# Two-layer hybrid encoder on one core: order of the branch projections, of the recurrence's levels and of the split-precision products

## The chip, the cores and the metric

The kernel runs on one core of a Trainium2 chip. The metric is the device time of one execution in microseconds (us). Engines are named as the profile names them: PE is the matrix engine (PEld its weight loads), DVE the vector engine, ACT the scalar engine, POOL the general-purpose engine, SP the engine that issues the weight transfers.

## The reference

256 tokens of width 1024 pass two layers. Each layer is: a half-step SwiGLU feed-forward (width 2816), a mixer, a second half-step feed-forward, each behind an RMS norm and with a residual add. The mixer, cut to what matters here:

```
z = h @ W_in            # u | q | f | v | out-gate (512 each) | branch gates (2 x 1024)
pool_out = pooling mixer of u        # 4 groups, windows 2, 4, 8, 16
o        = HGRN2 recurrence(q, f, v) # 4 heads, 128x128 state
hgrn_out = rmsnorm(o) * silu(out-gate)
merged = sigmoid(gA) * (pool_out @ w_pool_proj) + sigmoid(gB) * (hgrn_out @ w_hgrn_proj)
x = x + merged @ w_out
```

All of it is float32.

## The kernel before, in words

**Split products.** Every weight chunk (128 partitions x 2048 or 1408 columns of float32) is brought in by one transfer on SP's queue and split in two: ACT rounds it to `hi` (L116), DVE forms the rest `lo` = raw - hi (L117), each in two halves. Activations are split likewise, so that `x[:, 0]` is the rounded part and `x[:, 1]` the rest. A product of one 128x128 block is then two matmuls: `hi` against both parts of x at once (512 columns, L161) and `lo` against the rounded part (256 columns, L162). `mm_wide` issues this pair, so highs and lows alternate. `raw` has four buffers, `hi` and `lo` three each; `weights(key)` readies chunks up to two ahead of the one it returns.

**By tokens.** Value, out-gate, branch gates and the two branch projections are computed with tokens on the partitions (`by_tokens`, L185): for each of four k blocks and each half of the tokens (128), three matmuls of 512 columns (L192 to L194), into two accumulators, one for each half. A chunk is 24 matmuls.

**Stages of a layer.** Feed-forward: 22 gate/up chunks of 16 pairs, each followed by its evacuation into `hidden`, then 8 column blocks `j` of the down projection, 22 pairs each in two weight chunks. Mixer: f, v, q; then twelve steps (L606: two of the pool input u, two of the out-gate, eight of the branch gates), one weight chunk each; then the branch projections pp0, pp1, hp0, hp1 (`pp` for the pool branch, `hp` for the recurrence's, the number is the half of the 1024 columns); then the out-projection `wo`, whose first half takes k blocks 0 to 3 of four column blocks, then k blocks 4 to 7.

**Recurrence.** Eight parts: the first level, levels 2 to 64, and `across`. Each scales queries and keys on DVE (`decayed`, L463, L464), updates two decay tables on POOL (L466, L467), multiplies on PE (L484, L496, L510) into a tile of the two-buffer pool `gr`, and keeps a masked part (DVE L474). The scaled operands `m` have two buffers. Before, two parts stand ahead of each of the first four steps, and `outputs` (the final products L585, L587, norm, gate, and transposes L601 into the split tile `yhl`, for one half of the tokens after the other) ahead of step 5.

**From a branch projection to `wo`.** hp0 and hp1 yield, for each half of the tokens: z = ps * gate (L640), z += mg (L641, mg being the gated pp result, L632), four transposes (L601), a split (ACT L223, DVE L224). hp0 makes k blocks 0 to 3 of `merged`, hp1 k blocks 4 to 7.

**What sets the order.** A planner orders the instructions of each engine when the program is built: by priority, which is program order, among those that it holds ready. `urgent()` puts instructions 300 places ahead. So the order on an engine can depart from the order of the code; it is fixed once the program runs, and each engine then works strictly in it. Weight chunks come in the order of the list `stream` (L77).

Of the kernel before, what the change touches and what calls it, by code (L numbers as in the profile page):

```python
# [62 lines left out]
def _body(ctx, tc, a, out):  # L63
# [14 lines left out]
    for l in range(L):  # L78
        def ffn_chunks(f):
            for m in range(KF):  # L80
                stream.append(((f, l, "gu", m), a["gu"][l * 2 + f, m], CH))
            for j in range(KD):
                for h in range(2):
                    stream.append(((f, l, "dn", j, h), a["dn"][l * 2 + f, j][:, h * HALF:(h + 1) * HALF], HALF))
        ffn_chunks(0)
        for i in (0, 1):
            stream.append((("f", l, i), a["wi"][l, i], CH))
        def token_chunks(name, b):
            for i in (0, 1):
                stream.append(((name, l, i), a["wt"][l, b, i], CH))  # L90
        token_chunks("v", 0)
        for i in (2, 3, 4, 5):
            stream.append((("qu"[(i - 2) // 2], l, i % 2), a["wi"][l, i], CH))
        token_chunks("og", 1)
        for b in range(4):
            token_chunks(f"gate{b}", 2 + b)
        for name in ("pp", "hp"):
            for i in range(2):
                stream.append(((name, l, i), a[name][l, i], CH))
        for i in range(4):  # L100
            stream.append((("wo", l, i), a["wo"][l, i], CH))
        ffn_chunks(1)
# [55 lines left out]
    def mm_wide(ps, w, sl, x, start, stop):  # L158
# [2 lines left out]
        mm(ps, wh[:, sl], x, start=start, stop=False)  # L161
        mm(ps[:, 0], wl[:, sl], x[:, 0], start=False, stop=stop)  # L162

    def pair(w):

        pss = [pmm.tile([P, 2, S], F32, tag="mm", name="ps") for _ in range(2)]
        for k in range(KD):
            for g in range(2):
                c = (k * 2 + g) * P
                mm_wide(pss[g], w, slice(c, c + P), xs(k), k == 0, k == KD - 1)  # L170
        return pss

    def pair_sum(pss):
# [11 lines left out]
    def by_tokens(pss, w, x, ks, nk):  # L185

        wh, wl = w
        for i, k in enumerate(ks):
            sl = slice(i * 512, i * 512 + 512)
            for h in range(2):  # L190
                th = slice(h * P, h * P + P)
                mm(pss[h], x(k)[:, 0, th], wh[:, sl], start=k == 0, stop=False)  # L192
                mm(pss[h], x(k)[:, 0, th], wl[:, sl], start=False, stop=False)  # L193
                mm(pss[h], x(k)[:, 1, th], wh[:, sl], start=False, stop=k == nk - 1)  # L194
# [137 lines left out]
    def ffn(l, f, sq, gain):  # L332
        hs = slots(range(11), F32R)

        def hidden(k):
            return hs[k // 2].rearrange("p (k two) s -> p k two s", two=2)[:, k % 2]

        def gate_up(ms):
            ws = [weights((f, l, "gu", m)) for m in ms]
            pss = [[pmm.tile([P, 2, S], F32, tag="mm", name="ps") for _ in range(2)] for _ in ms]  # L340
            for k in range(0, KD, 2):
                for w, ps in zip(ws, pss):
                    for kk in (k, k + 1):
                        for g in range(2):
                            c = (kk * 2 + g) * P
                            mm_wide(ps[g], w, slice(c, c + P), xs(kk), kk == 0, kk == KD - 1)
            return list(zip(ms, pss))

        def evacuate(m, pss):
            z = pair_sum(pss)  # L350
            tt(out=z, in0=z, in1=bc(rb, 2), op=ALU.mult)  # L351
            s = tmp.tile([P, S], F32, tag="s", name="s")
            gate = nc.scalar.activation(s, z[:, 0], AF.Silu)  # L353
            h = tmp.tile([P, S], F32, tag="h", name="h")
            tt(out=h, in0=s, in1=z[:, 1], op=ALU.mult)  # L355
            split([hidden(m)[:, 0], hidden(m)[:, 1]], h)
            return gate

        n = FIRST if (l, f) == (0, 0) else 1
        groups = [range(n)] + [[m] for m in range(n, KF)]  # L360
        wait = gate_up(groups[0])
        with urgent():
            rc = norm_columns(sq)
        rb = None
        for ms in groups[1:]:
            wait += gate_up(ms)
            if rb is None:
                rb = norm_row(rc)
            for m, ps in wait:
                gate = evacuate(m, ps)  # L370
            wait = []
            if (f, m) == (0, 6):
                poolw = act.tile([P, NH, P], F32, tag="poolw", name="poolw")
                nc.sync.dma_start(out=poolw, in_=a["pw"][:, l])
                hnb = act.tile([P, 512], F32, tag="hnb", name="hnb")
                nc.sync.dma_start(out=hnb, in_=a["hnb"][:, l])
                pw.append((poolw, hnb))
            if (l, f, m) == (0, 0, 6):
                with tc.issue_after(gate.ins):
                    lower_bounds()  # L380
                nc.sync.dma_start(out=tab, in_=a["tab"])
        sq = Squares(gain is None)
        for j in range(KD):
            ps = pmm.tile([P, 2, S], F32, tag="mm", name="ps")
            wide = gain is not None or j < KD - 1
            for h in range(2):
                w = weights((f, l, "dn", j, h))
                for k in range(KF // 2):
                    kk = h * (KF // 2) + k
                    (mm_wide if wide else mm3)(  # L390
                        ps if wide else ps[:, 0], w, slice(k * P, k * P + P), hidden(kk), kk == 0, kk == KF - 1)
            if wide:
                with urgent():
                    nc.vector.scalar_tensor_tensor(  # L394
                        out=xT[:, j], in0=ps[:, 1], scalar=0.5, in1=xT[:, j], op0=ALU.mult, op1=ALU.add)
            residual(j, ps[:, 0], 0.5, gain, sq)
        return sq

    def mixer(l, sq, gain):
# [78 lines left out]

        def first_level():
            decayed(1, None, qx[:, :, P:].rearrange("p e (c n) -> p e c n", n=1))  # L480
            for q in range(NH):
                ps = pgr.tile([P, 2, 192], F32, tag="gr", name="gps")
                for g in range(2):
                    mm(ps[:, g], blocks(kk_)[:, 2 * q + g], qx[:, 2 * q + g], start=g == 0, stop=True,  # L484
                       skip_group_check=True)
                e = slice(2 * q, 2 * q + 2)
                tt(out=at_[:, e], in0=ps[:, :, 0:P], in1=ident.unsqueeze(1).broadcast_to([P, 2, P]), op=ALU.mult)
                keep(e, 1, ps[:, :, P:], P)

        def level(n):  # L490
            m = tmp.tile([P, 2 * NH, P], F32, tag="m", name="m")
            decayed(n, *halves(m, n))
            rows = P - n
            ps = pgr.tile([P, 2 * NH, 64], F32, tag="gr", name="gps")
            for e in range(2 * NH):
                mm(ps[0:rows, e], m[:, e, 0:rows], halves(m, n)[1][:, e], start=e == 0, stop=True,  # L496
                   skip_group_check=True)
            if n < 64:
                keep(slice(0, 2 * NH), n, ps[0:rows], rows)
            else:  # L500
                nc.scalar.copy(out=at_[0:64, :, 64:], in_=ps[0:64])

        def across():
            m = tmp.tile([P, 2 * NH, P], F32, tag="m", name="m")
            ml, mr = m[:, 0:NH], m[:, NH:]
            tt(out=ml, in0=kk_[:, :, 0:P], in1=suf[:, :, 0:P], op=ALU.mult)
            tt(out=mr, in0=queries.rearrange("p (h b) t -> p h b t", b=2)[:, :, 1], in1=pre[:, :, P:], op=ALU.mult)
            ps = pgr.tile([P, NH, P], F32, tag="gr", name="gps")
            for h in range(NH):
                mm(ps[:, h], ml[:, h], mr[:, h], start=h == 0, stop=True, skip_group_check=True)  # L510
            nc.scalar.copy(out=ax, in_=ps)


        up = act.tile([P, NH, PAD + S], F32, tag="up", name="up")
# [92 lines left out]
        steps += [lambda b=b, i=i: gate(b, i) for b in range(4) for i in range(2)]  # L607
        recur = [first_level] + [lambda n=n: level(n) for n in LEVELS[1:]] + [across]
        pools = [lambda g=g: pool_group(g) for g in range(NH)]
        for i, st in enumerate(steps):  # L610
            with urgent():
                for f in recur[2 * i:2 * i + 2]:
                    f()
                if i == 5:
                    outputs()
            st()
            if 3 <= i < 7:
# [9 lines left out]
        for b in range(2):  # L627
# [2 lines left out]
            by_tokens(pss, weights(("pp", l, b)), lambda k: part(phl, k), range(4), 4)  # L630
            for h in range(2):
                tt(out=mg[h][:, cols], in0=pss[h], in1=sg[h][:, cols], op=ALU.mult)  # L632
        for b in range(2):
            cols = slice(512 * b, 512 * b + 512)
            pss = token_tiles()
            by_tokens(pss, weights(("hp", l, b)), lambda k: part(yhl, k), range(4), 4)
            with urgent():
# [96 lines left out]
```

## Time and profile before

| | |
|---|---|
| median of 3 runs | 1105.19 us (1105.16 to 1106.74) |
| the profiled execution | 1106.67 us, its span 1104.9 us |
| PE busy | 1079.8 us (98%) |
| PEld busy | 937.1 us (85%) |
| DVE busy | 812.4 us (74%) |
| ACT busy | 573.3 us (52%) |
| POOL busy | 149.1 us (13%) |
| HBM read | 195.41 MB, 178 GB/s over the span |

A matmul's row lasts longer than its turn, since matmuls are pipelined: the distance from one start to the next is what it costs. "idle before" is the time that an engine sat without work, and the name behind the arrow is what ended it.

### The profile page before, as it was taken

The page shows a single profiled execution, that of the slowest core. Times are in us where ns is not written, and L with a number is a line of the kernel's source. Part 1 is how long each engine was busy: PE and PEld are TensorE (multiplying, and loading weights), DVE is VectorE, ACT ScalarE, POOL GpSimd, SP SyncE. Part 2 cuts the span into 40 slices and gives each one's busy share as a digit, 9 for nine tenths or more (in the row PEclk, how much of TensorE's full clock was granted, in tenths as well). Part 3 has the DMA queues.
Part 4 walks back from the last instruction along what each step waited for, and adds up shares of the span by engine and source line. Part 5 has one row for each costly group of instructions (what it writes and reads, how often), then busy time and mean ns, then how long its engine had stood idle before and what let it go on. Part 6 is the DMA issues. An engine that isn't in the chain of part 4 may idle for free.

```text
span 1104.9 us, 15670 instructions
## 1 busy us (share of the span) xinstructions
PE 1079.8 (98%) x6054; PEld 937.1 (85%) x6054; DVE 812.4 (74%) x1221; ACT 573.3 (52%) x984; POOL 149.1 (13%) x144
## 2 busy tenths in 40 slices
PE   8999999999998999999999999999999899999996
PEld 7888888888887888888888888888888688888885
DVE  8887766788656887776677776768985768777653
ACT  6665544643443665554555554446335446555541
POOL 5000001147200200000100000110751011000010
PEclk9999999999998999999999999999999989999998
DMA  9655466544434565546655544675434435554461
GB/s 339 240 183 179 147 188 229 204 153 163 152 128 149 193 214 189 178 135 187 241 198 184 188 155 132 210 266 191 153 120 163 175 115 197 190 191 154 140 197 38
DMA packets 33050, 197.46 MB, mean 179 GB/s; under 512 B 3792, under 2 KB 3920, under 8 KB 15824
## 3 DMA queue, kind: packets, MB, share of 16 engines
q1 hardware_dynamic: 32400, 195.84, 51.6%
q8 instruction: 47, 0.77, 0.3%
q10 hardware_dynamic: 576, 0.64, 0.2%
q14 instruction: 27, 0.22, 0.1%
HBM read 195.41 MB, written 1.05 MB: 178 GB/s over the span
## 4 chain that ended last, share of the span: by engine, by line
PE 85%; DVE 9%; issue 2%; POOL 1%; DMA 1%; ACT 0%; SPq 0%; POOLq 0%; DVEq 0%; ACTq 0%
PE ps L161 49%; PE ps L162 25%; DVE lo L117 5%; PE ps L192 3%; PE ps L193 3%; PE ps L194 3%; DVE m L464 1%; POOL b L467 1%; DMA xT<-in_x 1%; DMA raw<-in_gu 1%; POOL b L466 1%; DVE z L640 0%; DVE m L463 0%; PE gps L585 0%; PE gps L601 0%
## 5 line engine op out<-in xcount | busy, mean ns | idle before, releaser
L161 PE MATMUL ps<-xs__96,hi 128*128 128x512 f32 x1600 | 559.5, 395 | 3.1 <-DVE xs__96 L230 3.1
L117 DVE TENSOR_TENSOR lo<-raw,hi 128x1024 fp32r<-128x1024 f32 (+3 forms) x412 | 463.1, 1159 | 90.9 <-ACT hi L116 90.0
L116 ACT CAST hi<-raw 128x1024 fp32r<-128x1024 f32 (+3 forms) x412 | 374.2, 956 | 196.9 <-issue 81.1
L162 PE MATMUL ps<-xs__96,lo 128*128 128x256 f32 x1600 | 445.7, 280 | 0.0
L161 PEld LDWEIGHTS ps<-xs__96,hi 128*128 128x128 f32 x1600 | 299.3, 187 | 72.7 <-DVE xs__96 L230 4.3
L162 PEld LDWEIGHTS ps<-xs__96,lo 128*128 128x128 f32 x1600 | 301.6, 189 | 1.5 <-DVE lo L117 0.3
L161 PE MATMUL ps<-b,hi 128*128 128x512 f32 x810 | 287.5, 400 | 8.2 <-DVE b L224 8.2
L162 PE MATMUL ps<-b,lo 128*128 128x256 f32 x810 | 226.7, 281 | 0.0
L161 PEld LDWEIGHTS ps<-b,hi 128*128 128x128 f32 x810 | 153.9, 191 | 44.7 <-DVE b L224 8.6
L178 ACT COPY zl<-ps 128x256 f32<-128x256 f32 x200 | 73.4, 371 | 182.0 <-PE ps L162 181.2
L162 PEld LDWEIGHTS ps<-b,lo 128*128 128x128 f32 x810 | 154.7, 191 | 0.5
L253 POOL TENSOR_TENSOR acc<-acc,sq 128x256 f32<-128x256 f32 x48 | 46.9, 977 | 773.5 <-issue 517.7
L179 DVE TENSOR_TENSOR z<-ps,zl 128x256 f32<-128x256 f32 x200 | 83.0, 421 | 45.6 <-ACT zl L178 44.9
L193 PE MATMUL ps<-lo,xs__96 128*128 128x512 f32 x192 | 76.7, 400 | 0.0
L192 PE MATMUL ps<-hi,xs__96 128*128 128x512 f32 x192 | 75.4, 394 | 0.0
L194 PE MATMUL ps<-hi,xs__96 128*128 128x512 f32 x192 | 75.1, 391 | 0.0
L351 DVE TENSOR_TENSOR z<-z,rb 128x512 f32<-128x512 f32 x88 | 60.2, 686 | 0.6 <-ACT rb L284 0.5
L353 ACT ACTIVATE s<-z 128x256 f32<-128x256 f32 x88 | 36.7, 420 | 21.2 <-DVE z L351 21.1
L394 DVE SCALAR_TENSOR_TENSOR xT<-ps,xT 128x256 f32<-128x256 f32 x31 | 13.1, 424 | 45.5 <-PE ps L162 45.5
L223 ACT CAST b<-h 128x256 fp32r<-128x256 f32 x88 | 36.1, 411 | 13.4 <-DVE h L355 13.4
L192 PEld LDWEIGHTS ps<-hi,xs__96 128*128 128x128 f32 x192 | 36.1, 188 | 7.6
L194 PEld LDWEIGHTS ps<-hi,xs__96 128*128 128x128 f32 x192 | 36.1, 188 | 7.1
(123 smaller groups left out, 735.7 us busy)
## 6 DMA issues: line engine op xcount, KB each, us to landing
raw<-in_gu SPq DMA_DIRECT2D x82, 1024.0 KB, 4.8
raw<-in_dn SPq DMA_DIRECT2D x64, 704.0 KB, 4.1
raw<-in_wt SPq DMA_DIRECT2D x24, 1024.0 KB, 4.8
raw<-in_wi SPq DMA_DIRECT2D x12, 1024.0 KB, 4.8
raw<-in_wo SPq DMA_DIRECT2D x8, 1024.0 KB, 4.9
raw<-in_gu SPq DMA_DIRECT2D x8, 512.0 KB, 5.8
raw<-in_pp SPq DMA_DIRECT2D x4, 1024.0 KB, 4.8
raw<-in_hp SPq DMA_DIRECT2D x4, 1024.0 KB, 4.9
```

Source lines behind the costliest of these rows:

```text
L116: nc.scalar.copy(out=hi[:, sl], in_=raw[:, sl])
L117: tt(out=lo[:, sl], in0=raw[:, sl], in1=hi[:, sl].bitcast(F32), op=ALU.subtract)
L161: mm(ps, wh[:, sl], x, start=start, stop=False)
L162: mm(ps[:, 0], wl[:, sl], x[:, 0], start=False, stop=stop)
L178: nc.scalar.copy(out=zl[:, g], in_=pss[g][:, 1])
L179: tt(out=z[:, g], in0=pss[g][:, 0], in1=zl[:, g], op=ALU.add)
L192: mm(pss[h], x(k)[:, 0, th], wh[:, sl], start=k == 0, stop=False)
L193: mm(pss[h], x(k)[:, 0, th], wl[:, sl], start=False, stop=False)
L194: mm(pss[h], x(k)[:, 1, th], wh[:, sl], start=False, stop=k == nk - 1)
L253: nc.gpsimd.tensor_add(out=self.acc, in0=self.acc, in1=sq)
L351: tt(out=z, in0=z, in1=bc(rb, 2), op=ALU.mult)
L353: gate = nc.scalar.activation(s, z[:, 0], AF.Silu)
```

## The change

Four things are reordered; no product is added or taken away. The branch projections go pp0, hp0, pp1, hp1, in the code and in the order of the weight stream. `by_tokens` runs all k blocks of one half of the tokens, then the other half. `wide_run` issues all high products of a chunk and then all low ones; it is used by `pair` (f, q, u), by the down projection and by the gate/up chunks, but not by the first six chunks of the kernel's first feed-forward, and not by `wo`. In the recurrence each part is cut in a scaling and its products, and the products stand one step after the scaling: one part a step over steps 0 to 8, with `outputs` ahead of step 9.

```diff
-        for name in ("pp", "hp"):
-            for i in range(2):
+        for i in range(2):
+            for name in ("pp", "hp"):
                 stream.append(((name, l, i), a[name][l, i], CH))
...
+    def wide_run(w, tiles):
+
+        wh, wl = w
+        for ps, c, x, start, _ in tiles:
+            mm(ps, wh[:, c:c + P], x, start=start, stop=False)
+        for ps, c, x, _, stop in tiles:
+            mm(ps[:, 0], wl[:, c:c + P], x[:, 0], start=False, stop=stop)
...
-        for k in range(KD):
-            for g in range(2):
-                c = (k * 2 + g) * P
-                mm_wide(pss[g], w, slice(c, c + P), xs(k), k == 0, k == KD - 1)
+        wide_run(w, [(pss[g], (k * 2 + g) * P, xs(k), k == 0, k == KD - 1) for k in range(KD) for g in range(2)])
...
-        for i, k in enumerate(ks):
-            sl = slice(i * 512, i * 512 + 512)
-            for h in range(2):
-                th = slice(h * P, h * P + P)
+        for h in range(2):
+            th = slice(h * P, h * P + P)
+            for i, k in enumerate(ks):
+                sl = slice(i * 512, i * 512 + 512)
                 mm(pss[h], x(k)[:, 0, th], wh[:, sl], start=k == 0, stop=False)
...
+            if len(ms) == 1 and ((l, f) != (0, 0) or ms[0] > 5):
+                order = [(k, g) for k in range(KD) for g in range(2)]
+                wide_run(ws[0], [(pss[0][g], (k * 2 + g) * P, xs(k), k == 0, k == KD - 1) for k, g in order])
+                return list(zip(ms, pss))
...
+                kks = [(k, h * (KF // 2) + k) for k in range(KF // 2)]
+                if wide:
+                    wide_run(w, [(ps, k * P, hidden(kk), kk == 0, kk == KF - 1) for k, kk in kks])
+                    continue
...
+        products = None
         for i, st in enumerate(steps):
             with urgent():
-                for f in recur[2 * i:2 * i + 2]:
-                    f()
-                if i == 5:
+                if products:
+                    products()
+                products = recur[i]() if i < len(recur) else None
+                if i == 9:
                     outputs()
             st()
...
-        for b in range(2):
-            cols = slice(512 * b, 512 * b + 512)
             pss = token_tiles()
             by_tokens(pss, weights(("hp", l, b)), lambda k: part(yhl, k), range(4), 4)
```

## Rows read from the trace of the kernel before

**Rows 1.** The page: busy us, share of the span and instructions of each engine.

```profile
PE 1079.8 (98%) x6054; PEld 937.1 (85%) x6054; DVE 812.4 (74%) x1221; ACT 573.3 (52%) x984; POOL 149.1 (13%) x144
```

**Rows 2.** Groups by line, shapes apart: busy, mean ns, idle before and its releaser.

```profile
L161 PE MATMUL ps<-xs__96,hi 128*128 128x512 f32 x1600 | 559.5, 395 | 3.1 <-DVE xs__96 L230 3.1
...
L161 PE MATMUL ps<-b,hi 128*128 128x512 f32 x810 | 287.5, 400 | 8.2 <-DVE b L224 8.2
```

**Rows 3.** Windows: length, busy of PE, PEld, DVE, ACT, POOL, clock, DMA, GB/s.

```profile
336.00:341.60 5.60, 1.18 (x9) 0.71 (x7) 5.60 (x10) 2.83 (x5) 0.00 (x0) 0.86 0.73 263
341.60:347.00 5.40, 5.34 (x17) 4.56 (x18) 1.27 (x4) 0.41 (x2) 0.00 (x0) 0.51 0.52 194
```

**Rows 4.** Timeline of PE, hp1's end to wo: start, length, instruction, idle before.

```profile
335.93 0.60 PE L601 MATMUL gps<-cst,z 128*128 128x128 f32 x4
336.93 0.66 PE L601 MATMUL gps<-cst,z 128*128 128x128 f32 x4 [0.40 <-DVE z L641]
341.66 0.80 PE L161 MATMUL ps<-b,hi 128*128 128x512 f32 x1 [4.08 <-DVE b L224]
```

**Rows 5.** Timeline of DVE, the chain from hp0 to the split.

```profile
329.84 0.69 DVE L640 TENSOR_TENSOR z<-ps,b 128x512 f32<-128x512 f32 x1
...
342.11 0.76 DVE L224 TENSOR_TENSOR b<-gps,b 128x256 fp32r<-128x256 f32 x2
```

**Rows 6.** Timeline of PE: alternating pairs in two stretches.

```profile
599.99 0.40 PE L161 MATMUL ps<-xs__96,hi 128*128 128x512 f32 x1
...
601.75 0.40 PE L161 MATMUL ps<-xs__96,hi 128*128 128x512 f32 x1
...
1030.17 0.39 PE L161 MATMUL ps<-xs__96,hi 128*128 128x512 f32 x1
...
1031.21 0.39 PE L161 MATMUL ps<-xs__96,hi 128*128 128x512 f32 x1
```

**Rows 7.** Timeline of PE: a run of 512 columns, one of 256.

```profile
302.57 0.39 PE L192 MATMUL ps<-hi,xs__96 128*128 128x512 f32 x1
...
312.10 0.39 PE L192 MATMUL ps<-hi,xs__96 128*128 128x512 f32 x1
...
1089.58 0.28 PE L154 MATMUL ps<-b,hi 128*128 128x256 f32 x1
...
1090.30 0.28 PE L154 MATMUL ps<-b,hi 128*128 128x256 f32 x1
```

**Rows 8.** Timeline of PE, down projection: two highs, then two lows.

```profile
143.41 0.62 PE L161 MATMUL ps<-b,hi 128*128 128x512 f32 x2
143.88 0.40 PE L162 MATMUL ps<-b,lo 128*128 128x256 f32 x2
144.11 0.40 PE L161 MATMUL ps<-b,hi 128*128 128x512 f32 x1
```

**Rows 9.** Timeline of PE: the recurrence's two waits, the first product of the outputs.

```profile
266.08 1.76 PE L496 MATMUL gps<-m 128*112 128x64 f32 x16 [0.59 <-DVE m L464]
...
275.32 1.12 PE L496 MATMUL gps<-m 128*64 128x64 f32 x16 [0.83 <-DVE m L464]
...
289.43 1.05 PE L585 MATMUL gps<-vt,at__2284 128*128 128x128 f32 x8
```

**Rows 10.** Timeline of DVE: outputs' last split, out-gate's lows, the last input of a stage.

```profile
316.65 0.42 DVE L224 TENSOR_TENSOR b<-gps,b 128x256 fp32r<-128x256 f32 x1
...
246.78 2.06 DVE L117 TENSOR_TENSOR lo<-raw,hi 128x1024 fp32r<-128x1024 f32 x1
...
194.55 0.42 DVE L394 SCALAR_TENSOR_TENSOR xT<-ps,xT 128x256 f32<-128x256 f32 x1 [0.58 <-PE ps L162]
...
197.77 0.96 DVE L230 SCALAR_TENSOR_TENSOR xs__96<-xT,vec,xs__96 128x256 fp32r<-128x256 f32 x1
```

**Rows 11.** DVE by line in two windows, 243 to 272 and 60 to 120.

```profile
L117 DVE TENSOR_TENSOR lo<-raw,hi 128x1024 fp32r<-128x1024 f32 x8 | 15.2, 1923 | 0.0
...
L117 DVE TENSOR_TENSOR lo<-raw,hi 128x1024 fp32r<-128x1024 f32 x23 | 27.2, 1222 | 5.2 <-ACT hi L116 5.2
```

More of the change, by code (lines that the diff above doesn't have):

```diff
@@ L387, in ffn @@
                 w = weights((f, l, "dn", j, h))
[L388 to L391, printed above, removed]
+                kks = [(k, h * (KF // 2) + k) for k in range(KF // 2)]
+                if wide:
+                    wide_run(w, [(ps, k * P, hidden(kk), kk == 0, kk == KF - 1) for k, kk in kks])
+                    continue
+                for k, kk in kks:
+                    mm3(ps[:, 0], w, slice(k * P, k * P + P), hidden(kk), kk == 0, kk == KF - 1)
             if wide:
@@ L480, in first_level, with products @@
             decayed(1, None, qx[:, :, P:].rearrange("p e (c n) -> p e c n", n=1))
[L481 to L488, printed above, removed]
+            def products():
+                for q in range(NH):
+                    ps = pgr.tile([P, 2, 192], F32, tag="gr", name="gps")
+                    for g in range(2):
+                        mm(ps[:, g], blocks(kk_)[:, 2 * q + g], qx[:, 2 * q + g], start=g == 0, stop=True,
+                           skip_group_check=True)
+                    e = slice(2 * q, 2 * q + 2)
+                    tt(out=at_[:, e], in0=ps[:, :, 0:P], in1=ident.unsqueeze(1).broadcast_to([P, 2, P]),
+                       op=ALU.mult)
+                    keep(e, 1, ps[:, :, P:], P)
+            return products
         def level(n):
@@ L493, in level, with products @@
             rows = P - n
[L494 to L501, printed above, removed]
+            def products():
+                ps = pgr.tile([P, 2 * NH, 64], F32, tag="gr", name="gps")
+                for e in range(2 * NH):
+                    mm(ps[0:rows, e], m[:, e, 0:rows], halves(m, n)[1][:, e], start=e == 0, stop=True,
+                       skip_group_check=True)
+                if n < 64:
+                    keep(slice(0, 2 * NH), n, ps[0:rows], rows)
+                else:
+                    nc.scalar.copy(out=at_[0:64, :, 64:], in_=ps[0:64])
+            return products
         def across():
@@ L507, in across, with products @@
             tt(out=mr, in0=queries.rearrange("p (h b) t -> p h b t", b=2)[:, :, 1], in1=pre[:, :, P:], op=ALU.mult)
[L508 to L511, printed above, removed]
+            def products():
+                ps = pgr.tile([P, NH, P], F32, tag="gr", name="gps")
+                for h in range(NH):
+                    mm(ps[:, h], ml[:, h], mr[:, h], start=h == 0, stop=True, skip_group_check=True)
+                nc.scalar.copy(out=ax, in_=ps)
+            return products
         up = act.tile([P, NH, PAD + S], F32, tag="up", name="up")
```

## The prediction

> **What bounds the kernel now.** I read the page's busy shares first: PE is busy for 1079.8 of 1104.9 us [rows 1], so only two things can move the time much: PE's few gaps, and the distance from one matmul's start to the next. Second, the groups by line, for PE's gaps: the high products wait 3.1 us for xs, all of it at the very start, where nothing changes, and 8.2 us for the split L224 [rows 2]. Third, PE's timeline around that wait. It lies in each layer between the branch projections and `wo`. hp1's last matmul is issued just before 335.93; PE then has two sets of transposes with 0.40 us of waiting between them, and sits idle for 4.08 us until the first `wo` product at 341.66 [rows 4]. The windows show what follows: the granted clock is 0.86 while PE is idle and 0.51, which is the 1.2 GHz level, over the next 5.4 us [rows 3]. DVE's timeline says why `wo` waits: hp0's first z starts at 329.84, and the split that completes k blocks 0 to 3 starts at 342.11 [rows 5]. So hp0's evacuation takes 342.87 - 329.84 = 13.0 us, with weight lows in between, and only hp1 (24 matmuls of 0.227 us [rows 7], 5.4 us) stands as cover.
>
> **The order of the projections.** Price of the wait in one layer: 4.08 + 0.40 = 4.5 us idle. At half clock 17 matmuls took 5.4 us; 8.5 pairs at 0.352 us [rows 6] are 3.0 us, so 2.4 us are lost on top. Together 6.9 us, and 13.8 us in two layers. In the new order pp1 and hp1 (10.9 us) and eight transposes (1.3 us, from 0.60 + 0.66 in rows 4) lie between hp0 and `wo`: 12.2 us against a chain of 13.0 us. The chain also starts earlier, since an accumulator is now whole after half of its chunk: the first half of the tokens is ready 12 matmuls, 2.7 us, before hp0 ends. The wait should go. Late next is hp1's own evacuation, whose cover is `wo`'s first 16 pairs (16 x 0.35 = 5.6 us): for the second half of the tokens two DVE operations of 0.69 us, transposes of 0.6 us and a split of 0.76 us [rows 4, 5] make 2.7 us without lows between, and each pair of lows adds 2.4 us [rows 11]. I keep 0.5 us a layer for that, so -12.9 us. Bounds: nothing gained (the old wait comes back whole behind hp1) to -13.8 us.
>
> hp0 now needs `yhl` 5.4 us sooner. The last split of `yhl` starts at 316.65 [rows 10], done at 317.1. hp1 ended at 335.9, four projections of 24 x 0.227 us earlier is 314.1 (with the matmuls put in between, a little before); hp0 starts 5.4 us behind that, at 319.5, and needs the second half of the tokens at 322.3. There are 5 us to spare.
>
> **Highs, then lows.** 2186 pairs change order: 1312 of gate and up (88 chunks less 6, 16 each), 192 of f, q, u, and 682 of the down projections (4 x 8 x 22 less the 22 of the final block, which has another form). Alternating, the trace has two paces: 1.76 us for five pairs, 0.352 us each, and 1.04 us for three, 0.347 us [rows 6]; I take the mean of the two, 0.3495 us (an estimate: long stretches hold one pace or the other). After the change the nearest rows are runs of one width: 42 matmuls of 512 columns in 9.53 us, 0.2269 us, and six of 256 columns in 0.72 us, 0.120 us [rows 7]. Sum 0.3469 us, 2.6 ns less, times 2186 is -5.7 us. Both runs are of other operands; the same lines in a short run give 0.235 us for a high and 0.115 us for a low (two in 0.47, two in 0.23) [rows 8]. The ends are thus 0.2269 + 0.115 = 0.342 us (-16 us) and 0.235 + 0.120 = 0.355 us (+12 us). I take the long runs, because the new runs are 11 to 16 long.
>
> The Trainium skill ("TensorE: Matmul & The Clock Gate", Back-to-back issue gap) gives a warm distance that depends on the column count alone, about N/2.4 + 2.5 ns, so 216 ns and 109 ns. The trace differs from it (0.2269 and 0.120 us), and shows two paces for one mix. By that rule the order would be worth nothing, and the sum below would be 5.7 us higher.
>
> A run of highs also asks for its inputs sooner. At the turn from a down projection to the next stage, the last matmul ends at 194.5 and the last input, L230, at 198.73 [rows 10], 4.2 us later. In pairs the eighth k block comes after 14 pairs, 4.9 us; in highs after 14 x 0.232 = 3.2 us. PE would wait 1.0 us. But the planner fills such a place with lows: already now two highs and two lows stand in a row where the code alternates [rows 8]. `hidden` of the last chunk is asked for about 1.2 us sooner in the same way. Nine such turns, 0 to 1.1 us each: 0 to 10 us, and I take 1.5 us. Lows come due later than before, which costs nothing and gains nothing, as PE never waits for a low [rows 2].
>
> **By tokens.** The matmuls are the same. Only the second half of a chunk is asked for after 6 matmuls (1.4 us) and not after 12 (2.7 us). DVE is latest at the second out-gate chunk: its second low ends at 246.78 + 2.06 = 248.8 [rows 10], the chunk starts at about 246.3 (24 matmuls and a few inserted ones behind the first), so it was just in time and would now be 1.1 us late. 0 to 2.2 us in two layers; I take 1.0, as the planner may go on with highs.
>
> **The recurrence.** PE waits 0.59 and 0.83 us for the second of two levels that stand together [rows 9], 1.4 us a layer. A step holds about 30 to 42 instructions outside `urgent`, so 300 places are some eight steps: even the last part, now at step 7 or 8, still ranks ahead of all steps' weights, and the sequence of scalings and products among themselves is unaltered (scaling n+1 already followed products n). `outputs`, written at step 5, has its first product at 289.43 [rows 9], far behind that step's place, so its data sets it and not its step. I take 0, between -2.8 us (both waits go) and +2.8 (they double).
>
> The lows that lie beside POOL's updates take 1.92 us in place of 1.22 [rows 11], 0.7 us x 8 = 5.6 us of DVE time a layer. The Trainium skill ("SBUF — State Buffer", Who interferes with whom) says that a DVE instruction with two SBUF inputs and a POOL instruction that reads SBUF share a port by an exclusive lock. The rows agree; by that rule moving the levels moves these 5.6 us and removes none, which speaks against any gain from the recurrence's part.
>
> **Sum.** -12.9 - 5.7 + 1.5 + 1.0 + 0 = -16.1 us. The profiled execution took 1106.67 us (span 1104.9 and 1.8 around it) and would take 1090.6; it lies 1.5 us above the median of the runs, 1105.19. On the median: 1089.1 us.
>
> **Rivals.**
> A. The recurrence's waits go as well: 2.8 us less, 1086.3. For it: products now have a whole step behind their scaling. Against it: the ranking above.
> B. The planner holds `yhl` to be late, runs pp1 before hp0, and the old wait remains. 1105.2 - 5.7 + 2.5 = 1102.0. For it: the outputs' transposes stand at places that are later than their data. Against it: 5 us to spare.
> C. Slower: the recurrence really spreads to one part a step, and `yhl` becomes the wait. Its chain took 317.1 - 289.4 = 27.7 us. hp0 wants the second half at 322.3, so each us by which the outputs start after 294.6 is a us of waiting if the planner doesn't fill it; the gain of 6.4 us a layer is used up when they start after 301.0. Step 9's own place is at about 297; two recurrence parts late it is 305, which costs 10.4 us a layer, 2 x (10.4 - 6.4) = 8 us net, less 3.2 for the rest (-5.7 + 2.5): 1110.0.
> D. A run of lows is paced by its weight loads and a run of highs is no faster than in rows 8: +12 instead of -5.7, so 1106.8.
>
> **How the numbers follow.** Forecast 0.55, A 0.15, B 0.13, C 0.10, D 0.07. The forecast's own spread is some 5 us. Below 1079 would need most of the -16 us; above 1107 lie most of C and part of D, so 1079 to 1107 holds over 8 in 10. What this kernel's measurement can tell from no change is 0.2%, 2.2 us. Faster: the forecast, A, half of B and a little of the rest, 0.77; same: the other half of B and half of D, 0.10; slower: 0.13.
>
> **What would show it.** Right: no idle row ahead of `wo`'s first product, the clock at 1.00 across that window, PE rows of L161 and L162 in runs of 11 or 16, 0.227 to 0.23 us and 0.115 to 0.12 us apart; two short recurrence waits still there. Wrong: L161 still waiting for L224 by more than 1 us, or L192 waiting for L224 ahead of hp0 (C), or `hp` after pp1 (B). The prediction fails if the low runs stand at over 0.125 us apart, or if a new wait of several us appears at the mixer's steps.

## The result and the profile after

The changed kernel took 1093.12 us (median of 4 runs, 1092.60 to 1093.24) and the kernel before 1105.18 us (4 runs) beside it: ratio 0.9887, 95% interval 0.9870 to 0.9904. The prediction said 1089.1 us, with 1079 to 1107 as its range. The profiled execution took 1093.16 us with a span of 1091.4 us, 13.5 us less than before in both; the prediction had 16.1 us less.

The page after, busy time by engine, answers to [rows 1]. PE lost 6.9 us of busy time with the same instructions, and 13.5 us of span, so half of the gain is idle time that went.

```profile
PE 1072.9 (98%) x6054; PEld 937.3 (86%) x6054; DVE 807.3 (74%) x1221; ACT 580.5 (53%) x984; POOL 163.1 (15%) x144
```

The groups of PE by line, shapes apart (as in [rows 2]). The 8.2 us that `wo` (L161 on b) waited for the split are gone, the 3.1 us at the kernel's start are as they were, and the new lines of the runs (L168 high, L170 low) have a wait of 5.2 us for xs that no line had before.

```profile
L168 PE MATMUL ps<-xs__96,hi 128*128 128x512 f32 x1504 | 362.9, 391 | 5.2 <-DVE xs__96 L235 5.2
...
L161 PE MATMUL ps<-b,hi 128*128 128x512 f32 x128 | 45.0, 394 | 0.0
...
L161 PE MATMUL ps<-xs__96,hi 128*128 128x512 f32 x96 | 33.5, 400 | 3.1 <-DVE xs__96 L235 3.1
```

PE's timeline ahead of `wo` answers to [rows 4]: the transposes of the first half of `merged` now stand at 326.85 and 328.92, inside the projections, and the first `wo` product follows without idle time.

```profile
326.85 0.60 PE L622 MATMUL gps<-cst,z 128*128 128x128 f32 x4
328.92 0.60 PE L622 MATMUL gps<-cst,z 128*128 128x128 f32 x4
334.60 0.39 PE L161 MATMUL ps<-b,hi 128*128 128x512 f32 x1
```

The windows of the projections, of `wo`, and of the first 10 us of the second feed-forward (length, busy of PE, PEld, DVE, ACT, POOL, clock, DMA, GB/s) answer to [rows 3]. The clock stays at 1.00, the 2.4 GHz level, where the first 5.4 us of `wo` had run at 0.51. In the third window PE is busy for only 7.70 of 10.30 us: this is the new wait.

```profile
311.40:334.60 23.20, 23.20 (x110) 19.20 (x108) 17.96 (x24) 10.72 (x15) 0.00 (x0) 1.00 0.51 186
334.60:357.70 23.10, 23.10 (x137) 20.38 (x136) 16.70 (x27) 12.95 (x22) 4.64 (x4) 1.00 0.41 143
357.70:368.00 10.30, 7.70 (x33) 5.68 (x32) 8.84 (x14) 4.45 (x8) 5.20 (x4) 1.00 0.67 245
```

To see where the time went I took, in each trace, the start of the first matmul of every stage on PE; a stage lasts until the next one's first matmul. Both layers, in us (layer 1 / layer 2):

| stage | before | after | difference of both |
|---|---|---|---|
| first feed-forward, gate/up | 126.0 / 124.6 | 126.1 / 122.9 | -1.6 |
| its down projection | 62.0 / 61.2 | 61.3 / 61.3 | -0.6 |
| mixer up to pp0 | 119.4 / 119.2 | 117.3 / 117.3 | -4.0 |
| branch projections | 28.0 / 28.0 | 23.2 / 23.2 | -9.6 |
| `wo` | 25.9 / 25.8 | 23.1 / 23.1 | -5.5 |
| second feed-forward, gate/up | 122.8 / 122.7 | 126.2 / 126.2 | +6.9 |
| its down projection, layer 1 | 61.0 | 61.3 | +0.3 |

The sum is -14.1; the stretch ahead of the first row is 0.3 us longer, and what comes behind layer 2's gate/up takes up the rest to the span's -13.5. So 15.1 us were won between pp0 and the end of `wo`, and nearly half of that was given back one stage later.

The place of the new wait, PE and then DVE. The highs of three chunks stand in front, as far as their inputs are there: 6, a wait, 14, a wait, 17; the first low comes at 369.41. DVE had no idle time between 348 and 357.7 and makes xs between residuals (L320, L677) and weight lows (L117).

```profile
357.74 1.55 PE L168 MATMUL ps<-xs__96,hi 128*128 128x512 f32 x6
360.31 3.49 PE L168 MATMUL ps<-xs__96,hi 128*128 128x512 f32 x14 [1.03 <-DVE xs__96 L235]
365.38 4.19 PE L168 MATMUL ps<-xs__96,hi 128*128 128x512 f32 x17 [1.58 <-DVE xs__96 L235]
369.41 0.76 PE L170 MATMUL ps<-xs__96,lo 128*128 128x256 f32 x5
```

```profile
359.79 0.47 DVE L235 SCALAR_TENSOR_TENSOR xs__96<-xT,vec,xs__96 128x256 fp32r<-128x256 f32 x1
...
361.57 2.89 DVE L117 TENSOR_TENSOR lo<-raw,hi 128x1024 fp32r<-128x1024 f32 x2
364.39 0.94 DVE L235 SCALAR_TENSOR_TENSOR xs__96<-xT,vec,xs__96 128x256 fp32r<-128x256 f32 x1
```

The recurrence on PE answers to [rows 9]. Its levels stand alone, each with time behind its scaling, and no wait is left; between them all four products of the pooling groups (L563) have come in ahead of the outputs (L606, 293.01). Before, the last two of the four (L542) stood behind the outputs' last transposes (L601); the second fence shows them.

```profile
264.77 1.79 PE L513 MATMUL gps<-m 128*120 128x64 f32 x16
269.68 0.59 PE L563 MATMUL gps<-pd,poolw 128*128 128x256 f32 x2
271.73 1.69 PE L513 MATMUL gps<-m 128*112 128x64 f32 x16
278.10 0.59 PE L563 MATMUL gps<-pd,poolw 128*128 128x256 f32 x2
...
284.95 0.59 PE L563 MATMUL gps<-pd,poolw 128*128 128x256 f32 x2
...
285.70 1.15 PE L513 MATMUL gps<-m 128*64 128x64 f32 x16
...
293.01 1.06 PE L606 MATMUL gps<-vt,at__2284 128*128 128x128 f32 x8
```

```profile
312.33 0.60 PE L601 MATMUL gps<-cst,b 128*128 128x128 f32 x4
312.76 0.60 PE L542 MATMUL gps<-pd,poolw 128*128 128x256 f32 x2
...
318.67 0.59 PE L542 MATMUL gps<-pd,poolw 128*128 128x256 f32 x2
```

### The profile page after: what moved, and what is told of

Same layout as the page of the kernel before. It is cut to its first block, busy times and chain, and to the rows that moved or that the text cites. A ratio compares the mean times of both kernels' runs of the same rounds, so it can differ in the third digit from the quotient of the medians.

```text
span 1091.4 us, 15703 instructions
## 1 busy us (share of the span) xinstructions
PE 1072.9 (98%) x6054; PEld 937.3 (86%) x6054; DVE 807.3 (74%) x1221; ACT 580.5 (53%) x984; POOL 163.1 (15%) x144
## 4 chain that ended last, share of the span: by engine, by line
PE 93%; DVE 3%; issue 2%; DMA 1%; ACT 0%; POOLq 0%; POOL 0%; DVEq 0%; SPq 0%; ACTq 0%
PE ps L168 45%; PE ps L170 24%; PE ps L197 5%; PE ps L198 5%; PE ps L199 5%; PE ps L161 3%; PE gps L513 2%; PE ps L162 2%; DVE lo L117 1%; DVE xs__96 L235 1%; PE gps L622 0%; PE gps L497 0%; DMA xT<-in_x 0%; DVE xT L320 0%; DMA vec<-in_vec 0%
## 5 line engine op out<-in xcount | busy, mean ns | idle before, releaser
L117 DVE TENSOR_TENSOR lo<-raw,hi 128x1024 fp32r<-128x1024 f32 (+3 forms) x412 | 457.5, 1148 | 172.2 <-ACT hi L116 125.8
L168 PE MATMUL ps<-xs__96,hi 128*128 128x512 f32 x1504 | 362.9, 391 | 5.2 <-DVE xs__96 L235 5.2
L168 PEld LDWEIGHTS ps<-xs__96,hi 128*128 128x128 f32 x1504 | 275.7, 188 | 59.8 <-DVE xs__96 L235 6.9
L170 PEld LDWEIGHTS ps<-xs__96,lo 128*128 128x128 f32 x1504 | 194.3, 191 | 8.0
L170 PE MATMUL ps<-xs__96,lo 128*128 128x256 f32 x1504 | 197.4, 283 | 0.0
L168 PE MATMUL ps<-b,hi 128*128 128x512 f32 x682 | 166.3, 391 | 0.0
L168 PEld LDWEIGHTS ps<-b,hi 128*128 128x128 f32 x682 | 124.1, 189 | 23.1
L170 PEld LDWEIGHTS ps<-b,lo 128*128 128x128 f32 x682 | 89.9, 191 | 4.9
L170 PE MATMUL ps<-b,lo 128*128 128x256 f32 x682 | 91.4, 282 | 0.0
L183 ACT COPY zl<-ps 128x256 f32<-128x256 f32 x200 | 64.5, 367 | 9.8 <-PE ps L162 7.7
L161 PE MATMUL ps<-b,hi 128*128 128x512 f32 x128 | 45.0, 394 | 0.0
L198 PEld LDWEIGHTS ps<-lo,xs__96 128*128 128x128 f32 x192 | 36.1, 188 | 7.0
```

The lines of the kernel that those rows point to most:

```text
L117: tt(out=lo[:, sl], in0=raw[:, sl], in1=hi[:, sl].bitcast(F32), op=ALU.subtract)
L168: mm(ps, wh[:, c:c + P], x, start=start, stop=False)
L170: mm(ps[:, 0], wl[:, c:c + P], x[:, 0], start=False, stop=stop)
L183: nc.scalar.copy(out=zl[:, g], in_=pss[g][:, 1])
```

## The experiments

Diffs named "from after" undo or alter something in the changed kernel, those "from before" add one thing to the old one. The kernel before was run beside each of them; its median was 1105.87 to 1105.99 us.

### What removes the wait ahead of `wo`

**The order undone** (from after; code and weight stream).

```diff
-        for i in range(2):
-            for name in ("pp", "hp"):
+        for name in ("pp", "hp"):
+            for i in range(2):
...
+        for b in range(2):
+            cols = slice(512 * b, 512 * b + 512)
```

> The changed kernel with the branch projections, and their weights, in the old order pp0, pp1, hp0, hp1. Theory (cover): the wait of wo's first products for L224 comes back, though shorter, since with the tokens half by half hp0's first accumulator is whole 2.7 us sooner: 4.5 - 2.7 = 1.8 us idle a layer and perhaps no slow clock behind it, so +4 us (1097); at most the old 6.9 us a layer, +14 (1107). Rival (halves): the half-by-half order alone removed the wait and the order of the projections is worth nothing: 1093 +- 1.

Measured: 1091.79 us, ratio 0.9872 (0.9855 to 0.9888). The old order costs nothing here: the projections take 24.5 us (1.3 us more: two short waits of 0.30 and 0.21 us ahead of `wo`, and a third set of transposes that stands there in place of inside `wo`), `wo` 22.8, and the second gate/up 124.5 in place of 126.2. The order is not needed for the gain.

**The recurrence undone** (from after).

```diff
-                if products:
-                    products()
-                products = recur[i]() if i < len(recur) else None
-                if i == 9:
+                for f in recur[2 * i:2 * i + 2]:
+                    f()()
+                if i == 5:
```

> The changed kernel with the recurrence as before: two parts a step over steps 0 to 3, scaling and products together, outputs ahead of step 5. Theory (spread): the two waits of PE for m (0.59 + 0.83 us a layer) come back, as two levels stand together again: +2.8 to +3.7 us, 1096.3. Rival (as predicted): the cut in scaling and products doesn't matter, and the waits went for another reason: 1093 +- 1.

Measured: 1091.69 us, 0.9871 (0.9856 to 0.9886). Neither is this part. The mixer takes 117.5 us in place of 117.3, as only one of the two waits of the recurrence is left, 0.24 us long.

**By tokens undone** (from after: k blocks outside, halves of the tokens inside).

```diff
-        for h in range(2):
-            th = slice(h * P, h * P + P)
-            for i, k in enumerate(ks):
+        for i, k in enumerate(ks):
...
+            for h in range(2):
+                th = slice(h * P, h * P + P)
```

> The changed kernel with by_tokens as before (both halves of the tokens for each k block). Theory (halves): most of the gain at wo comes from an accumulator being whole after half a chunk. Then hp1's evacuation of both halves starts only at its end and wo's 16 pairs (5.6 us) don't cover it: a wait of 1 to 4 us a layer for L229 comes, +2 to +8 us, 1095 to 1101. Rival (order): pp1 and hp1 as cover for hp0 are what counts, no wait over 0.5 us at wo: 1093 +- 1.

Measured: 1094.04 us, 0.9897 (0.9884 to 0.9910). No wait ahead of `wo`; the stages to the end of `wo` are as in after (23.2 and 23.4 us), and the turn into the second gate/up (the passage from one stage to the next) waits 2.9 us a layer, where after waits 2.6. So far any single part could be missed. The next six take the parts one or two at a time.

**Only the order** (from before; the first of these diffs, reversed).

> The kernel before with the order pp0, hp0, pp1, hp1 alone. Theory (halves): hp0's evacuation is covered, hp1's isn't; of 6.9 us a layer at wo 3 to 6 are won, -6 to -12 us, 1094 to 1100. Theory (order): all 13.8 us are won, 1092.

Measured: 1098.90 us (1095.70 to 1100.99, 6 runs), 0.9936 (0.9917 to 0.9955). The order alone removes the wait ahead of `wo`: projections and `wo` take 28.0 + 25.9 us before and 23.2 + 24.2 us here, and 12.6 us less in both layers. What is left is a wait of 0.8 us a layer, 8.9 us behind the first `wo` product. The second gate/up gives 3.5 and 1.0 us back.

```profile
PE ps L161 <- DVE b L227: 1.6, 2, 0.8
```

**Only the halves by tokens** (from before; the diff above, reversed), and **halves and runs** (from before: the same and `wide_run` as in the change; order and recurrence as before).

> The kernel before with by_tokens half by half alone. Theory (halves): as with the old order in the changed kernel, 0.8 us a layer of waiting is left at wo and the clock stays at 1.00: -12 us, 1094. Rival (order): the wait is only 2.7 us shorter, the clock still falls: -5 us, 1101. The recurrence's waits (1.4 us a layer) stay in both.

> By_tokens half by half and the runs of highs and lows, with the projections' order and the recurrence as before. Theory: the two parts left out are worth nothing by themselves (without the order -1.6 us against the changed kernel, without the recurrence's part -1.8), as what they win is lost again at wo and at the turn to the second feed-forward: 1090 to 1092 us. Rival (each part pays where it stands): without both, the waits at wo (0.8 us a layer) and for m (1.4 us a layer) stand together: 1096.

Measured: 1105.53 us, 0.9997 (0.9987 to 1.0006), and 1103.61 us, 0.9980 (0.9972 to 0.9989). Both keep the wait: PE's list of waits (total us, times, longest) has the same first line as before but for the line's number (8.2 us, as in [rows 2]), here of the second kernel.

```profile
PE ps L161 <- DVE b L229: 8.2, 2, 4.1
```

At this point my theory was that the late pooling groups were the cause: two levels at a time hold both buffers of `gr`, so groups 2 and 3 come behind the outputs, mg (L632) is formed only from 325 on, and hp0's evacuation queues behind it on DVE [rows 5]. Four kernels tested it.

```profile
325.01 2.05 DVE L632 TENSOR_TENSOR b<-ps,b 128x512 f32<-128x512 f32 x3 [4.72 <-PE ps L194]
```

**Only the recurrence** (from before; its part of the change).

> The kernel before with nothing but the recurrence's part of the change (one part a step, its products a step behind their scaling). Theory: the wait ahead of wo comes from the last two groups of the pooling mixer, which stand behind the outputs because the recurrence's products, two levels together, keep both buffers of the tile pool gr; levels one by one let all four groups in ahead of the outputs, so the wait (6.9 us a layer with the half clock) goes without any change of the projections' order, and the two waits of the recurrence (1.6 us a layer) go too: 1105.5 - 13.8 - 3.2 = 1088.5 us, up to 1095 if the pairs' pace or a turn takes some of it. Rival: the order of the projections is needed for it, only the recurrence's waits go: 1102 us, with the wait of 4 us at wo still there.

**Only the pooling groups early** (from before; one line).

```diff
-            ps = pgr.tile([P, 512], F32, tag="gr", name="gps")
+            ps = pmm.tile([P, 512], F32, tag="mm", name="gps")
             mm(ps[:, :S], pw[l][0][:, g], d, start=True, stop=True)
```

> The kernel before with one line changed: the pooling groups' product goes into a buffer of the five-buffer pool mm in place of one of the two of gr. Recurrence, order, pairs as before. Theory (late pool groups are the cause): all four groups run before the outputs, mg is formed before the recurrence's branch is, and the wait ahead of wo goes, while the recurrence's two waits stay: 1105.5 - 13.8 = 1091.7 us, up to 1097 if pace or turns take some. Rival (the cover of one chunk behind hp0 is what is short, as the prediction had it): the wait of 4 us stays, 1104.5 to 1106.5 us.

**Pooling groups late** (from after with the order undone as above, and this on top).

```diff
-            if 3 <= i < 7:
-                pools[i - 3]()
+            if i in (3, 4, 10, 11):
+                pools[(3, 4, 10, 11).index(i)]()
```

> The kernel after with the projections' order of before (which alone took 1091.8 us) and with the last two pooling groups put behind steps 10 and 11, so behind the outputs, where they stood before. Theory (late pool groups are the cause): the wait ahead of wo is back, 3 to 5 us a layer and the half clock behind it: 1098 to 1105 us. Rival (the recurrence's spread itself, or the highs' runs, removes the wait): 1092 us plus or minus 1, no wait over 1 us ahead of wo.

**Pooling groups early and runs** (from before: the one line of the early groups, and `wide_run` as in the change).

> Highs and then lows as in the kernel after, pooling groups in the pool mm, and nothing else: order of the projections, by tokens and recurrence as before. Theory: 1091.5 us plus or minus 1.5, as fast as the kernel after with a third of its edits, since the two other parts do no more than let mg be formed early. Rival (the other parts carry a gain of their own): 1097 us or more.

Measured, in this order: 1103.07 us, 0.9976 (0.9966 to 0.9987); 1109.14 us, 1.0027 (1.0014 to 1.0040); 1102.97 us, 0.9973 (0.9962 to 0.9984); 1112.54 us, 1.0062 (1.0047 to 1.0077). Half of my theory fell. The buffers of `gr` do hold the groups back: with their product in another pool the last group stands at 282.9, ahead of the outputs at 284.9. With the groups late the wait is back, as the theory said, but with the groups early and nothing else it stays, and is longer. PE's lists of waits, of the recurrence alone, of the groups early, and of the groups late:

```profile
PE ps L161 <- DVE b L227: 10.2, 2, 5.1
```

```profile
PE ps L161 <- DVE b L224: 10.2, 2, 5.1
PE gps L496 <- DVE m L464: 4.2, 4, 1.3
```

```profile
PE ps L161 <- DVE b L229: 8.1, 2, 4.1
```

The runs of this section together give a rule without an exception:

| order new | groups ahead of the outputs | halves by tokens | longest wait at `wo`, us |
|---|---|---|---|
| no | no | no (before) / yes (halves only, halves and runs, groups late) | 4.1 |
| no | yes | no (recurrence only, groups early, groups early and runs) | 5.1 |
| no | yes | yes (order undone) | 0.3 |
| yes | no | no (order only) / yes (recurrence undone) | 0.8 / 0.7, both behind its first products |
| yes | yes | no (by tokens undone) / yes (after) | 0 |

In the old order it thus takes both early groups and halves, as far as these runs go: the one kernel with both has the runs of highs and the recurrence's part as well, and early groups with halves and nothing else were not run. DVE's timelines of two kernels with early groups, one without halves and one with them (and with the runs of highs), say why. First the recurrence alone: both halves of hp0 are complete only at its end, so z (L661) starts at 329.20; the next z waits 1.72 us for hp0's transposes, which stand behind hp1 on PE; and the splits (L227) come last, behind hp1's z's and two lows.

```profile
329.20 1.37 DVE L661 TENSOR_TENSOR z<-ps,b 128x512 f32<-128x512 f32 x2 [1.27 <-PE ps L197]
...
335.76 1.29 DVE L661 TENSOR_TENSOR z<-ps,b 128x512 f32<-128x512 f32 x2 [1.72 <-PE gps L620]
...
340.44 1.61 DVE L227 TENSOR_TENSOR b<-gps,b 128x256 fp32r<-128x256 f32 x4
```

```profile
335.13 1.04 PE L620 MATMUL gps<-cst,z 128*128 128x128 f32 x8
341.24 0.79 PE L161 MATMUL ps<-b,hi 128*128 128x512 f32 x1 [5.08 <-DVE b L227]
```

Then the kernel with the order undone, with halves: the first z is at 326.37, its transposes are let in before hp1 ends, and the splits (L229) stand between the z's.

```profile
326.37 0.69 DVE L663 TENSOR_TENSOR z<-ps,b 128x512 f32<-128x512 f32 x1
...
333.54 0.41 DVE L229 TENSOR_TENSOR b<-gps,b 128x256 fp32r<-128x256 f32 x1
...
335.40 0.41 DVE L229 TENSOR_TENSOR b<-gps,b 128x256 fp32r<-128x256 f32 x1
```

```profile
332.29 0.60 PE L622 MATMUL gps<-cst,z 128*128 128x128 f32 x4
...
335.87 0.50 PE L161 MATMUL ps<-b,hi 128*128 128x512 f32 x1 [0.21 <-DVE b L229]
```

The recurrence alone also shows its own worth: its two waits (2.8 us in both layers, [rows 9]) are gone, and the mixer is 1.1 and 1.2 us shorter. The time is 2.9 us less, but the part of that beyond the mixer's 2.3 us comes from other stages, where the pairs' pace differs (in its trace the first gate/up of layer 2 is 1.9 us shorter, the last down projection of layer 1 is 1.0 us longer). With the groups early and the old recurrence those waits grow from 0.59 and 0.83 us to 0.76 and 1.31 us. Why the groups early with runs is the slowest of all is not settled: it has the long wait ahead of `wo`, waits of up to 1.8 us in the recurrence and 1.2 us at the turn, and a mixer of 121.1 and 122.2 us.

### What the runs of highs cost and bring

**Pairs again** (from after: `wide_run` issues the pairs of `mm_wide`).

```diff
-        for ps, c, x, start, _ in tiles:
-            mm(ps, wh[:, c:c + P], x, start=start, stop=False)
-        for ps, c, x, _, stop in tiles:
-            mm(ps[:, 0], wl[:, c:c + P], x[:, 0], start=False, stop=stop)
+        for ps, c, x, start, stop in tiles:
+            mm_wide(ps, w, slice(c, c + P), x, start, stop)
```

> The changed kernel with alternating pairs in place of runs of highs and lows everywhere. Theory: the turn's waits go (-5.5 us), and the pace goes from 0.3486 us a pair (runs, 0.229 + 0.1195 by the changed kernel's trace) back to between 0.3467 and 0.353 by stretch, mean 0.349: +1 us for 2186 pairs. Sum -4.5 us, 1088.6. Rival (runs pay): runs are quicker by 2.6 ns a pair as predicted, +5.7 - 5.5: 1093.

Measured: 1094.33 us, 0.9895 (0.9880 to 0.9910). The wait at the turn shrinks to 0.34 us, although DVE makes xs no sooner (L233 at 360.33 and 364.92, against 359.79 and 364.39 in after): pairs ask for it later.

```profile
360.85 0.50 PE L161 MATMUL ps<-xs__96,hi 128*128 128x512 f32 x1 [0.34 <-DVE xs__96 L233]
```

But the pairs are slower. From one matmul's start to the next, over all highs and lows of the kernel with waits left out, a pair takes 234.6 + 116.2 = 350.8 ns here and 229.1 + 119.2 = 348.3 ns in after; over 2410 pairs that is 6.0 us. The waits behind highs (what their distances hold above 245 ns) are 4.7 us fewer. So by the traces the runs are worth 6.0 - 4.7 = 1.3 us. The times differ by 1.2 us, which is less than this measurement can tell.

**Only the first three chunks of each second feed-forward in pairs** (from after).

```diff
-            if len(ms) == 1 and ((l, f) != (0, 0) or ms[0] > 5):
+            if len(ms) == 1 and (ms[0] > 2 if f == 1 else l == 1 or ms[0] > 5):
```

> The changed kernel with one thing undone: the first three gate/up chunks of each second feed-forward are issued in alternating pairs again. Theory (turn): in the changed kernel PE waits about 1.0 and 1.6 us per layer there for L235, because the low products of an accumulator can't go before its high ones, so that only 0.227 us per block lie between one xs and the next in place of 0.347 us. Then both waits go in both layers: -5.2 to -5.9 us, 1087.5 us, and L168's idle for L235 falls from 5.2 us to under 1. Rival (DVE): xs comes late because DVE is full there, and the wait only moves to the next chunk: 1092 to 1093 us.

Measured: 1091.91 us, 0.9874 (0.9859 to 0.9889). The wait for xs shrank to 0.34 us a layer, as the theory had it, but a new one of 1.57 us a layer stands 25 us later, in the first runs, for the evacuation of a chunk on ACT. So the second gate/up is 0.5 us a layer shorter than in after (125.7 in place of 126.2 us) and the span 1.4 us, not 5.

```profile
PE ps L168 <- ACT b L228: 3.1, 2, 1.6
```

Three versions (order undone, recurrence undone, first chunks in pairs) are 1.2 to 1.4 us below the changed kernel, which is less than what this measurement can tell; that they ran on the same chip as it is not on record.

## Why the prediction was nearly right

**The size.** Forecast -16.1 us, measured -13.5 us on the profiled executions. The median's miss is larger, 4.0 us, because the profile of before lay 1.5 us above its median and that of after on it. That the sum came so near is in part luck: the turns cost 4.3 us more than forecast and the runs of highs brought 3.3 us less, while the projections and `wo` won 2.2 us more, `by_tokens` cost nothing where 1.0 us was kept for it, and the mixer got shorter where nothing was forecast.

**Order of the projections, -12.9 us.** Right for the order alone: -12.6 us between pp0 and the end of `wo`. The sign that it named came true: no idle row ahead of `wo`'s first product, and the clock at 1.00 in its window. The whole change won 15.1 us there: with the groups early the 0.7 to 0.8 us of waiting inside `wo` go too (`wo` 24.3 us with the recurrence undone, 23.1 in after); that the mg operations, then out of DVE's way, are the reason is likely and not shown. One reading was too long. The prediction took the chain behind hp0 to the last split at 342.11, 13.0 us; the split that let PE go is the one before it, done at 341.61, so the chain is 11.8 us, and the new order's 12.2 us cover it.

```profile
340.85 0.76 DVE L224 TENSOR_TENSOR b<-gps,b 128x256 fp32r<-128x256 f32 x2
```

What the prediction did not see is that the order is one of two remedies. It held the short cover behind hp0 for the cause; with the cover as short as before, halves and early groups, in the company of the other parts, remove the wait as well (1091.79 us with the order undone). It did name the halves' 2.7 us as a help; by themselves they are worth nothing.

**Runs of highs, -5.7 us.** This term was mis-sized: 348.3 ns a pair, where 346.9 was forecast. Runs of 16 highs and 16 lows in after follow each other every 5.57 us (347.9 ns a pair, in every gate/up stage).

```profile
623.63 3.82 PE L168 MATMUL ps<-xs__96,hi 128*128 128x512 f32 x16
627.28 2.08 PE L170 MATMUL ps<-xs__96,lo 128*128 128x256 f32 x16
629.20 3.82 PE L168 MATMUL ps<-xs__96,hi 128*128 128x512 f32 x16
```

16 highs take 627.28 - 623.63 = 3.65 us, 228 ns each (forecast 227), and 16 lows 1.92 us, 120 ns each (forecast 120): both within rounding, but 1.4 ns too little in the sum. More weighs what was replaced. The mean of before, 349.5 ns, was right (349.3 measured over all), so the kernel gains 2410 x 1.0 = 2.4 us over all pairs, but in the second gate/up the pairs had stood at the faster pace, 346.7 ns, and the runs lose 1.2 ns x 704 = 0.8 us there.

**The turns, +1.5 us.** The step that failed: "But the planner fills such a place with lows". It filled it with highs of the next chunks; in the order it laid, no low of an accumulator stands ahead of its highs, and three chunks' accumulators were open when xs ran out. The cost is 1.03 + 1.58 us of idle time in layer 1 and 1.03 + 1.60 in layer 2, 5.2 us, and 5.8 us from start to start. It fell at one turn of the nine, from `wo` to the second gate/up, where DVE is behind; the turn that the prediction worked out (down projection to the next stage) waits for nothing.

**By tokens, +1.0 us.** Nothing was measured: -0.3 us, within the interval. The out-gate's low did not come late.

**The recurrence, 0 us.** Wrong, in the direction of rival A: "even the last part, now at step 7 or 8, still ranks ahead of all steps' weights" is not how it came out. The last level's products went from 275.32 to 285.70, each level by itself, and the outputs' first product from 289.43 to 293.01. The waits of 2.8 us went, against the prediction's sign that two short ones would still be there. In the kernel with that edit alone the mixer is 2.3 us shorter; in the company of the other parts the edit is worth nothing measurable, since halves and runs without it leave one wait of 0.24 us a layer and a mixer of 117.5 us (117.3 in after). Rival C's point was 294.6 us for the outputs' start, so 293.01 was near: `hp0` still waits for nothing.

**The other rivals.** B: the code's order held. D: lows in runs are 120 ns apart, below the 125 that it wanted.

By stages, the difference is -15.1 (projections and `wo`) - 4.0 (mixer) - 2.2 (first feed-forward) + 6.9 (second gate/up, 5.8 of it the turn) + 0.3 (its down projection) = -14.1 us, the table's sum. The mixer's 4.0 us can't be given to one part: the recurrence's part alone wins 2.3 us there, halves and runs without it 3.6 us.

## What to carry to other kernels

When PE stops waiting for a busy helper engine in one stage, look which of its inputs that engine makes for the next stage, because the time may be asked for again there (15.1 us won here, 5.8 us lost one stage later). Highs first makes a chunk ask for all its inputs in two thirds of the time (229 of 348 ns a pair), so it belongs where the inputs are ready long before. Before crediting one part of a change, run it alone, and run the change without it: here 12.6 to 13.1 us between pp0 and the end of `wo` were won with the order alone, and also by the other parts without the order.

## What the runs showed of the hardware

Alternating pairs have two sharp paces. In 20 us windows of before, of the order alone and of the recurrence alone, the mean is 346.7 ns or 353.3 ns, in some windows a mix, and a stretch of 100 us and more holds one of them. The same lines with operands of the same shapes have either, so these alone do not choose it. Between 419.62 and 423.78 before makes 12 pairs in 4.16 us; the kernel with pairs again makes 11 in 3.89 us, both at a granted clock of 1.00, the 2.4 GHz level. The Trainium skill ("TensorE: Matmul & The Clock Gate", Back-to-back issue gap) gives a warm distance by the column count alone, for a matmul taken by itself; these traces show two for the same counts.

```profile
419.62 0.39 PE L161 MATMUL ps<-xs__96,hi 128*128 128x512 f32 x1
...
423.78 0.39 PE L161 MATMUL ps<-xs__96,hi 128*128 128x512 f32 x1
```

```profile
419.75 0.40 PE L161 MATMUL ps<-xs__96,hi 128*128 128x512 f32 x1
...
423.64 0.40 PE L161 MATMUL ps<-xs__96,hi 128*128 128x512 f32 x1
```

In these windows the pace changes at waits and stage bounds. In layer 1's second gate/up the kernels with the wait ahead of `wo` and pairs stand at 346.7 ns from 400 us on (before, halves only, recurrence only, groups early), the two without it and with pairs (order only, pairs again) at 353.3 ns: 22 x 16 pairs x 6.6 ns = 2.3 us a layer. In that stage the kernels without the wait so lose a part of what its removal brought, and the runs, which hold 347.9 ns in every gate/up stage, bring some of it back. That the wait sets the pace is not shown, and what does was not found: in layer 2 the order alone, without the wait, stands at 346.7 ns, and pairs again at 353.3 ns.
